# Grouping two high and two low matrix products at a few fixed places of every GEMM

## The chip, the cores and the metric

The kernel runs on one core of a Trainium2 chip. The metric is the device time of one execution in microseconds. Of the core's engines four matter here: TensorE, whose products are called PE and whose weight loads are called PEld in the profile; VectorE (DVE); ScalarE (ACT); and SyncE (SP), which issues the transfers of the weights.

## The reference

The reference computes one transformer-like block on 256 tokens of width 2048, in float32. Cut to its matrix products it is this:

```python
h = h + 0.5 * swiglu(rmsnorm(h, ffn1_norm), ffn1_w_in, ffn1_w_out)     # 2048 -> 2*5632 -> 2048
h = h + hybrid_mixer(rmsnorm(h, mix_norm), mix_w_in, ..., mix_w_out)   # 2048 -> 11296, 4096 -> 2048
h = h + 0.5 * swiglu(rmsnorm(h, ffn2_norm), ffn2_w_in, ffn2_w_out)
gate = sigmoid(rmsnorm(h, ple_norm) @ ple_w_gate)                      # 2048 -> 2048
h = h + gate * (p @ ple_w_proj)                                        # 256 -> 2048
return rmsnorm(h, final_norm)
```

Inside the mixer there are short convolutions, a gate and a state-space scan in two chunks of 128 tokens; their products are few beside those of the large weights.

## The kernel before, in words

Activations lie with the features on the 128 partitions and the 256 tokens along the row. Every float32 operand of a large product is split in two numbers of the type fp32r: a high part, which is the operand rounded, and a low part, which is what the rounding left over. An activation tile has the high part in columns 0 to 255 and the low part in columns 256 to 511 (the tiles `xa`, `xb`, `ga`, `gb`, `ya`, `yb`). A weight tile is split by the function `parts` into two tiles, `hi` (ScalarE copies, line 99) and `lo` (VectorE subtracts, line 100), for KC = 4 contraction tiles of 128 rows and 256 output columns at a time; such a piece is called a chunk.

The class `Gemm` does all large products. Its accumulator `acc` has two banks, one for each half j of the 256 output columns. For one contraction tile k and one half j there are two products, and each loads its own 128 by 128 weights first:

- the high product, `hi` weights times all 512 columns of the activation tile, into the 512 columns of the bank;
- the low product, `lo` weights times the 256 high columns, into the bank's columns 256 to 511.

The helper `gather` adds the two halves of the bank afterwards. The method `chunk` walks j on the outside and the four k inside, so TensorE sees a high and a low product in strict alternation, a pair for each k. One `Gemm` over 16 contraction tiles has 32 pairs. In the whole program there are 6,384 such pairs: 88 calls over 16 tiles in the two feed-forward input products, 44 in the mixer's input product, one of half width for dt, 48 calls over 15 or 14 tiles in the feed-forward output products, 8 over 32 tiles in the mixer's output product and 7 over 16 tiles in the gate. In a last gate tile and in the small product `pr` (the argument `one`), the products are all 256 columns wide: high weights times the high columns, high weights times the low columns, low weights times the high columns.

Between calls stand a few small products in plain float32: `nps` sums a norm over the partitions (four products with one moving column, line 183), and `npb` spreads the result over the partitions (four products, line 210).

A scheduler orders the instructions of each engine by the program and by priorities; `parts` has a raised priority. TensorE takes its instructions in that order.

Of the kernel before, what the change touches and what calls it, by code (L numbers as in the profile page):

```python
# [15 lines left out]
T = 256  # L16
# [9 lines left out]
KC = 4  # L26
# [23 lines left out]
def block_kernel(ctx, tc, xT, pT, small, dtp, w1, o1, wm, wdt, om, w2, o2, wg, wp, out):  # L50
    nc = tc.nc
# [11 lines left out]
    def aux(name):  # L63
        return aux_p.tile([P, 512], F32, tag="aux", name=name)
# [28 lines left out]
    def parts(src, nk, cols):  # L93
        w = raw.tile([P, KC, 256], F32, tag="w", name="w")
        nc.sync.dma_start(out=w[:, :nk, :cols], in_=src)
        hi = wsp.tile([P, KC, 256], F32R, tag="hi", name="hi")
        lo = wsp.tile([P, KC, 256], F32R, tag="lo", name="lo")
        with tc.high_priority(44):
            A.copy(out=hi[:, :nk, :cols], in_=w[:, :nk, :cols])  # L99
            V.tensor_tensor(out=lo[:, :nk, :cols], in0=w[:, :nk, :cols],  # L100
                            in1=hi[:, :nk, :cols].bitcast(F32), op=ALU.subtract)
        return hi, lo

    class Gemm:

        def __init__(self, src, K, rhs, cols=256, one=False, acc=None):
            self.src, self.K, self.rhs, self.cols, self.one = src, K, rhs, cols, one
            self.acc = acc_p.tile([P, 2, 512], F32, tag="acc", name="acc") if acc is None else acc  # L110

        def chunk(self, k0, k1):
            hi, lo = parts(self.src[:, k0:k1, :], k1 - k0, self.cols)
            for j in range(self.cols // P):
                js = slice(j * P, (j + 1) * P)
                for k in range(k0, k1):
                    x, acc = self.rhs(k), self.acc[:, j, :]
                    wh, wl = hi[:, k - k0, js], lo[:, k - k0, js]
                    if self.one:
                        todo = [(acc[:, 0:T], wh, x[:, 0:T]), (acc[:, 0:T], wh, x[:, T:]),  # L120
                                (acc[:, 0:T], wl, x[:, 0:T])]
                    else:
                        todo = [(acc, wh, x), (acc[:, T:], wl, x[:, 0:T])]
                    for n, (o, a, b) in enumerate(todo):
                        nc.tensor.matmul(o, lhsT=a, rhs=b, start=(k == 0 and n == 0),  # L125
                                         stop=(k == self.K - 1 and n == len(todo) - 1))

        def all(self):
            for k0 in range(0, self.K, KC):
# [3 lines left out]
    def gemm(*args, **kw):  # L133
        return Gemm(*args, **kw).all()
# [167 lines left out]
    n, held = 0, []  # L302
# [179 lines left out]
    for g in range(GROUPS):  # L482
        ng = Norm(512, "rg")
        for a in range(2):
            j = 4 * g + 2 * a
# [39 lines left out]
    for m in range(0, KD, 2):  # L525
        tail = m == KD - 2
        proj = lambda: gemm(wp[m // 2], 2, lambda k: px[:, k, :], one=True,
                            acc=aux("pr").rearrange("p (j t) -> p j t", j=2))
        pr = proj() if tail else None
        for q in range(2 if tail else 1):  # L530
            n = 1 if tail else 2
            acc = gemm(wg[m // 2][:, :, q * P:(q + n) * P], KD, xp, cols=n * P, one=tail)
# [98 lines left out]
```

## Time and profile before

| what | value |
|---|---|
| time, median of 3 executions | 2347.32 us (2345.47 to 2348.5) |
| time of the profiled execution | 2349.11 us |
| its span, first to last instruction | 2347.4 us |
| mean granted TensorE clock | 0.998 |
| TensorE products (PE) busy | 2328.8 us, 99% of the span, 13,340 products |
| weight loads (PEld) busy | 2014.5 us, 86% |
| VectorE busy | 1508.3 us, 64% |
| ScalarE busy | 1133.4 us, 48% |
| transfers | 429.38 MB, mean 183 GB/s |

The profiled execution's time is 1.7 us more than its span, and 1.8 us above the median. Products are pipelined: one starts before the one ahead of it has ended, so the ends overlap in the trace and the busy share of PE says only that some product was always in flight. What a product costs is read as the distance from its start to the next one's start.

### The profile page before, as it was taken

Reading aid. Unit: us, or ns where it says so; the run is one execution under the profiler, and the core shown is the slowest. Engines: PE = TensorE matmul, PEld = TensorE weight load, DVE = VectorE, ACT = ScalarE, POOL = GpSimd, SP = SyncE. Lnnn points to the kernel's source line nnn. Section 1 sums busy time; section 2 is a strip of 40 time slices with the busy share of each in tenths; the row PEclk is TensorE's granted clock in tenths of the full one; section 3 lists DMA queues with packets and bytes.
Section 4 is the critical chain, followed back from the end, with each engine's and each line's share of the span. In section 5 each row is a group of like instructions: output and inputs, shape, how many; then the busy total and the mean of one; then the engine's idle time right before and its main releaser. Section 6 shows DMA issues by size and latency. Waiting matters only on the chain.

```text
span 2347.4 us, 33616 instructions
## 1 busy us (share of the span) xinstructions
PE 2328.8 (99%) x13340; PEld 2014.5 (86%) x13340; DVE 1508.3 (64%) x1928; ACT 1133.4 (48%) x1491; POOL 11.8 (1%) x25
## 2 busy tenths in 40 slices
PE   8999999999999999999999999999999999999998
PEld 7888888888888888888888888888888888888887
DVE  7665566556667777777777655566556655666765
ACT  6444444444455555444455444444444444444553
POOL 0000000000000000000000000000000000000000
PEclk9999999999999999999999999999999999999999
DMA  7666666666666555555555666666666666666654
GB/s 237 187 186 181 190 187 187 182 189 187 188 180 191 185 184 178 158 165 163 170 169 179 186 186 184 186 185 186 186 188 187 185 186 186 189 185 180 189 182 137
DMA packets 126862, 429.38 MB, mean 183 GB/s; under 512 B 13616, under 2 KB 20016, under 8 KB 126704
## 3 DMA queue, kind: packets, MB, share of 16 engines
q1 hardware_dynamic: 126144, 426.17, 60.4%
q8 instruction: 104, 1.70, 0.3%
q10 hardware_dynamic: 480, 0.80, 0.1%
q14 instruction: 54, 0.44, 0.1%
q0 software_dynamic: 80, 0.26, 0.0%
HBM read 425.08 MB, written 2.10 MB: 182 GB/s over the span
## 4 chain that ended last, share of the span: by engine, by line
PE 99%; DVE 0%; DMA 0%; issue 0%; POOL 0%; ACT 0%; POOLq 0%; DVEq 0%
PE acc L125 97%; PE pr L125 0%; PE yp L407 0%; PE yp L410 0%; PE ab L386 0%; DMA sm<-in_small 0%; PE npb L210 0%; PE xt L362 0%; PE st L375 0%; PE nps L183 0%; POOL hw L559 0%; DVE cv L294 0%; DVE lo L100 0%; PE cb L355 0%; DVE xa L152 0%
## 5 line engine op out<-in xcount | busy, mean ns | idle before, releaser
L100 DVE TENSOR_TENSOR lo<-w,hi 128x1024 fp32r<-128x1024 f32 (+1 forms) x834 | 991.1, 1189 | 735.2 <-ACT hi L99 728.5
L99 ACT CAST hi<-w 128x1024 fp32r<-128x1024 f32 (+1 forms) x834 | 851.2, 1021 | 1054.2 <-PE acc L125 851.9
L125 PE MATMUL acc<-xa,hi 128*128 128x512 f32 (+1 forms) x2264 | 804.9, 399 | 6.3 <-DVE xa L152 6.3
L125 PE MATMUL acc<-xb,hi 128*128 128x512 f32 (+1 forms) x2264 | 800.8, 397 | 0.0
L125 PE MATMUL acc<-xb,lo 128*128 128x256 f32 x2248 | 633.3, 282 | 0.0
L125 PE MATMUL acc<-xa,lo 128*128 128x256 f32 x2248 | 632.3, 281 | 0.8 <-DVE lo L100 0.8
L125 PEld LDWEIGHTS acc<-xa,hi 128*128 128x128 f32 x2264 | 425.4, 188 | 110.8 <-ACT hi L99 6.3
L125 PEld LDWEIGHTS acc<-xb,hi 128*128 128x128 f32 x2264 | 424.3, 188 | 102.8
L125 PEld LDWEIGHTS acc<-xb,lo 128*128 128x128 f32 x2248 | 424.6, 189 | 3.1 <-issue 2.9
L125 PEld LDWEIGHTS acc<-xa,lo 128*128 128x128 f32 x2248 | 425.8, 189 | 1.7 <-DVE lo L100 1.5
L125 PE MATMUL acc<-ga,hi 128*128 128x512 f32 x768 | 273.7, 399 | 0.0
L125 PE MATMUL acc<-gb,hi 128*128 128x512 f32 x640 | 228.1, 398 | 0.0
L125 PE MATMUL acc<-ga,lo 128*128 128x256 f32 x768 | 215.8, 281 | 0.0
L125 PE MATMUL acc<-gb,lo 128*128 128x256 f32 x640 | 179.6, 281 | 0.0
L125 PEld LDWEIGHTS acc<-ga,hi 128*128 128x128 f32 x768 | 144.3, 188 | 35.9
L125 PEld LDWEIGHTS acc<-gb,hi 128*128 128x128 f32 x640 | 120.3, 188 | 30.2
L125 PEld LDWEIGHTS acc<-ga,lo 128*128 128x128 f32 x768 | 145.1, 189 | 0.0
L141 DVE SCALAR_TENSOR_TENSOR esum<-acc,elo 128x512 f32<-128x512 f32 (+1 forms) x196 | 133.7, 682 | 0.0
L125 PEld LDWEIGHTS acc<-gb,lo 128*128 128x128 f32 x640 | 120.9, 189 | 0.0
L139 ACT ACTIVATE elo<-acc 128x512 f32<-128x512 f32 (+1 forms) x196 | 115.5, 590 | 0.0
L125 PE MATMUL acc<-ya,hi 128*128 128x512 f32 x256 | 90.9, 399 | 0.0
L125 PE MATMUL acc<-yb,hi 128*128 128x512 f32 x256 | 90.9, 399 | 0.0
(142 smaller groups left out, 1133.5 us busy)
## 6 DMA issues: line engine op xcount, KB each, us to landing
w<-in_w SPq DMA_DIRECT2D x350, 512.0 KB, 4.4
w<-in_wm SPq DMA_DIRECT2D x176, 512.0 KB, 4.3
w<-in_o SPq DMA_DIRECT2D x144, 512.0 KB, 3.6
w<-in_om SPq DMA_DIRECT2D x64, 512.0 KB, 3.6
w<-in_wg SPq DMA_DIRECT2D x28, 512.0 KB, 4.6
w<-in_o SPq DMA_DIRECT2D x32, 384.0 KB, 3.6
w<-in_o SPq DMA_DIRECT2D x16, 256.0 KB, 3.5
w<-in_wp SPq DMA_DIRECT2D x8, 256.0 KB, 2.6
```

The source lines that it names most:

```text
L99: A.copy(out=hi[:, :nk, :cols], in_=w[:, :nk, :cols])
L100: V.tensor_tensor(out=lo[:, :nk, :cols], in0=w[:, :nk, :cols], in1=hi[:, :nk, :cols].bitcast(F32), op=ALU.subtract)
L125: nc.tensor.matmul(o, lhsT=a, rhs=b, start=(k == 0 and n == 0), stop=(k == self.K - 1 and n == len(todo) - 1))
L139: A.mul(out=lo[:, :n, :], in_=acc[:, :n, T:], mul=scale)
L141: V.scalar_tensor_tensor(out=s[:, :n, :], in0=acc[:, :n, 0:T], scalar=scale, in1=lo[:, :n, :], op0=ALU.mult, op1=ALU.add)
```

## The change

The order of the products inside a chunk is given by a string, H for the next high product and L for the next low one. As a rule it is HLHL..., as before. For the first half of the output columns (j = 0) in full chunks of four contraction tiles, it is HHLLHHLL where the chunk begins at a contraction tile divisible by 16, and HHLLHLHL where it begins 8 tiles later. The k of each product is counted separately for H and L, so the same products are summed into the same accumulator, in another order. The marks of the first and the last product of an accumulation go to the first and the last of the list.

```diff
-                for k in range(k0, k1):
-                    x, acc = self.rhs(k), self.acc[:, j, :]
-                    wh, wl = hi[:, k - k0, js], lo[:, k - k0, js]
+                order = "HL" * (k1 - k0)
+                if j == 0 and k1 - k0 == KC:
+                    order = {0: "HHLLHHLL", 8: "HHLLHLHL"}.get(k0 % 16, order)
+                todo, acc, nh, nl = [], self.acc[:, j, :], k0, k0
+                for part in order:
+                    if part == "H":
+                        k, w, nh = nh, hi, nh + 1
+                    else:
+                        k, w, nl = nl, lo, nl + 1
+                    x, a = self.rhs(k), w[:, k - k0, js]
...
-                        todo = [(acc, wh, x), (acc[:, T:], wl, x[:, 0:T])]
-                    for n, (o, a, b) in enumerate(todo):
-                        nc.tensor.matmul(o, lhsT=a, rhs=b, start=(k == 0 and n == 0),
-                                         stop=(k == self.K - 1 and n == len(todo) - 1))
+                        todo.append((acc[:, T:], a, x[:, 0:T]))
+                for n, (o, a, b) in enumerate(todo):
+                    nc.tensor.matmul(o, lhsT=a, rhs=b, start=(k0 == 0 and n == 0),
+                                     stop=(k1 == self.K and n == len(todo) - 1))
```

On TensorE, this is the start of the second `Gemm` of the program's main part (the first feed-forward tile after the norm's spread `npb`), as it stood before; xa is the activation tile of contraction tiles 0 to 7, hi_402 and lo_403 are the weights of the first chunk.

```order
L210 MATMUL npb_382<-ident_87,nrt_348 128x128 x2
L125 MATMUL acc_399<-xa_104,hi_402 128x512
L125 MATMUL acc_399<-xa_104,lo_403 128x256
L125 MATMUL acc_399<-xa_104,hi_402 128x512
L125 MATMUL acc_399<-xa_104,lo_403 128x256
L125 MATMUL acc_399<-xa_104,hi_402 128x512
```

The same place in the changed kernel, where x2 means two such products one behind the other:

```order
L220 MATMUL npb_382<-ident_87,nrt_348 128x128 x2
L135 MATMUL acc_399<-xa_104,hi_402 128x512 x2
L135 MATMUL acc_399<-xa_104,lo_403 128x256 x2
L135 MATMUL acc_399<-xa_104,hi_402 128x512 x2
L135 MATMUL acc_399<-xa_104,lo_403 128x256 x2
L135 MATMUL acc_399<-xa_104,hi_402 128x512
L135 MATMUL acc_399<-xa_104,lo_403 128x256
```

Two groups of two high and two low products now stand at the head of the call; the alternation goes on behind them with the second half of the columns. There are 608 such groups in the program.

On VectorE a few rows near the start of the dt product (the stretch about 897 us into the span) stand in another order. Before, with cv the convolution's tile and lo the low weights:

```order
L294 SCALAR_TENSOR_TENSOR cv<-esum,sm,cv 128x255
L294 SCALAR_TENSOR_TENSOR cv<-esum,sm,cv 128x253
L294 SCALAR_TENSOR_TENSOR cv<-esum,sm,cv 128x254
L100 TENSOR_TENSOR lo<-w,hi 128x1024
L294 SCALAR_TENSOR_TENSOR cv<-esum,sm,cv 128x253
```

In the changed kernel at that place:

```order
L324 TENSOR_TENSOR esum<-esum,r 128x512
L100 TENSOR_TENSOR lo<-w,hi 128x1024
L304 SCALAR_TENSOR_TENSOR cv<-esum,sm,cv 128x255 x2
L304 SCALAR_TENSOR_TENSOR cv<-esum,sm,cv 128x254 x2
```

The low weights are now made ahead of the convolution's multiplications and no longer between them. SyncE's and GpSimd's instructions stand in the same order in both kernels.

## Rows read from the trace of the kernel before

**Rows 1.** Page: span; busy time of TensorE; its granted clock in 40 slices.

```profile
span 2347.4 us, 33616 instructions
PE 2328.8 (99%) x13340; PEld 2014.5 (86%) x13340; DVE 1508.3 (64%) x1928; ACT 1133.4 (48%) x1491; POOL 11.8 (1%) x25
PEclk9999999999999999999999999999999999999999
```

**Rows 2.** Page: the chain that ended last, by engine.

```profile
PE 99%; DVE 0%; DMA 0%; issue 0%; POOL 0%; ACT 0%; POOLq 0%; DVEq 0%
```

**Rows 3.** Waits of TensorE: who waited for whom, us in total, times, longest.

```profile
PE acc L125 <- DVE xa L152: 6.3, 1, 6.3
...
PE acc L125 <- DVE lo L100: 0.8, 1, 0.8
```

**Rows 4.** Timeline of TensorE from 778.8 us: start, duration, instruction.

```profile
778.82 0.60 PE L210 MATMUL npb<-ident,nrt 128*128 128x128 f32 x4
...
779.97 0.40 PE L125 MATMUL acc<-xa,hi 128*128 128x512 f32 x1
780.21 0.28 PE L125 MATMUL acc<-xa,lo 128*128 128x256 f32 x1
780.33 0.40 PE L125 MATMUL acc<-xa,hi 128*128 128x512 f32 x1
780.56 0.28 PE L125 MATMUL acc<-xa,lo 128*128 128x256 f32 x1
780.68 0.40 PE L125 MATMUL acc<-xa,hi 128*128 128x512 f32 x1
780.91 0.28 PE L125 MATMUL acc<-xa,lo 128*128 128x256 f32 x1
781.03 0.40 PE L125 MATMUL acc<-xa,hi 128*128 128x512 f32 x1
```

**Rows 5.** Timeline of TensorE from 767.2 to 778.5 us.

```profile
767.27 0.50 PE L183 MATMUL nps<-ones,nacc 128*128 128x1 f32 x4
767.63 0.48 PE L125 MATMUL acc<-xa,hi 128*128 128x512 f32 x1
767.95 0.28 PE L125 MATMUL acc<-xa,lo 128*128 128x256 f32 x1
768.07 0.40 PE L125 MATMUL acc<-xa,hi 128*128 128x512 f32 x1
768.30 0.28 PE L125 MATMUL acc<-xa,lo 128*128 128x256 f32 x1
768.42 0.39 PE L125 MATMUL acc<-xa,hi 128*128 128x512 f32 x1
768.65 0.27 PE L125 MATMUL acc<-xa,lo 128*128 128x256 f32 x1
768.76 0.40 PE L125 MATMUL acc<-xa,hi 128*128 128x512 f32 x1
...
778.47 0.40 PE L125 MATMUL acc<-xb,hi 128*128 128x512 f32 x1
```

**Rows 6.** Line 125 by stretches: us, busy and count of products, of loads, PEclk, transfers.

```profile
32.90:767.16 734.26, 734.26 (x4158) 636.74 (x4156) 1.00 0.62 186
...
1242.84:1253.59 10.75, 10.75 (x63) 9.47 (x62) 1.00 0.62 192
1254.39:1265.33 10.94, 10.94 (x63) 9.49 (x62) 1.00 0.49 147
...
1506.30:2240.80 734.50, 734.50 (x4159) 636.88 (x4158) 1.00 0.63 186
```

**Rows 7.** Timeline of TensorE from 2320 us, in the small product `pr`.

```profile
2320.07 0.40 PE L125 MATMUL pr<-px,hi 128*128 128x256 f32 x2
2320.31 0.28 PE L125 MATMUL pr<-px,lo 128*128 128x256 f32 x1
2320.43 0.40 PE L125 MATMUL pr<-px,hi 128*128 128x256 f32 x2
```

More of the change, by code (lines that the diff above doesn't have):

```diff
@@ L115, in chunk @@
                 js = slice(j * P, (j + 1) * P)
-                for k in range(k0, k1):
-                    x, acc = self.rhs(k), self.acc[:, j, :]
-                    wh, wl = hi[:, k - k0, js], lo[:, k - k0, js]
+                order = "HL" * (k1 - k0)
[8 more added lines that the diff above has]
+                    x, a = self.rhs(k), w[:, k - k0, js]
                     if self.one:
-                        todo = [(acc[:, 0:T], wh, x[:, 0:T]), (acc[:, 0:T], wh, x[:, T:]),
-                                (acc[:, 0:T], wl, x[:, 0:T])]
-                    else:
-                        todo = [(acc, wh, x), (acc[:, T:], wl, x[:, 0:T])]
-                    for n, (o, a, b) in enumerate(todo):
-                        nc.tensor.matmul(o, lhsT=a, rhs=b, start=(k == 0 and n == 0),
-                                         stop=(k == self.K - 1 and n == len(todo) - 1))
+                        todo += [(acc[:, 0:T], a, x[:, i:i + T]) for i in ((0, T) if part == "H" else (0,))]
+                    elif part == "H":
+                        todo.append((acc, a, x))
+                    else:
+                        todo.append((acc[:, T:], a, x[:, 0:T]))
+                for n, (o, a, b) in enumerate(todo):
+                    nc.tensor.matmul(o, lhsT=a, rhs=b, start=(k0 == 0 and n == 0),
+                                     stop=(k1 == self.K and n == len(todo) - 1))
         def all(self):
```

## The prediction

> **What bounds the kernel now.** I read the page first. A product is in flight for 99% of the span, and the granted clock is full in every slice [rows 1]. The chain of waits lies to 99% on TensorE [rows 2]. The table of waits then says whether TensorE starves: its longest wait for tiles of the large products is 6.3 us, once, at the start, and it waited for low weights 0.8 us, once [rows 3]. So neither transfers nor ScalarE nor VectorE sets the time; only the distance from one product's start to the next does. A product more or less in another engine is worth nothing, and a nanosecond per pair is worth 6.4 us over the 6,384 pairs.
>
> That distance is read from the timeline, and the reader should see that it has two patterns. From 779.97 us three pairs take 781.03 - 779.97 = 1.06 us: the highs start 0.36, 0.35 and 0.35 us apart, and this goes on with period three [rows 4]. The mean is 353.3 ns; I call it the long beat. From 768.07 to 778.47 us thirty pairs take 10.40 us, 346.7 ns each; the highs start 0.35 and 0.34 us apart in turn, period two [rows 5]. This is the short beat. The same instructions, tiles and clock stand in both. Lined up by stretches: 734.26 us with 4,158 products, two of which began before the stretch, are 2,078 pairs of 353.3 ns; the stretch from 1506 us gives the same; a mixer tile of 31 pairs takes 10.75 us at 1242 us (346.8 ns) and the next one 10.94 us (353 ns, the first pairs still settling) [rows 6].
>
> A beat, once begun, lasts until something else than the alternation goes through TensorE: 2,078 pairs without a change [rows 6]. What changes it is a short interruption. Behind the four `nps` products the short beat follows [rows 5], eight times of eight in the timeline; behind the four `npb` products the long one [rows 4], nine times of nine. Transfers differ between neighbouring stretches without order (192 and 147 GB/s, [rows 6]), and the pattern does not react to what VectorE or ScalarE begin beside it. So the beat looks like a state of TensorE's own pipeline, entered by the phase in which a run of alternating products begins. What the mechanism is, no row says.
>
> **The change, part by part.** It adds and removes no instruction; 608 groups HHLL replace two pairs each. Three prices follow.
>
> (a) The group itself. Inside it two neighbours are new: high after high, low after low. The trace of before has neither for these widths. A high product is followed after 0.23 us at least [768.42 to 768.65, rows 5] and 0.24 us at most [779.97 to 780.21, rows 4]; a low one after 0.11 us [768.65 to 768.76, rows 5] to 0.12 us. For low after low the nearest row is the small product: products of 256 columns into the same columns, three in 0.36 us, 0.12 us each whichever weights they have [rows 7]. So a group takes between 2 x 0.23 + 2 x 0.11 = 0.68 us and 2 x 0.24 + 2 x 0.12 = 0.72 us, against 0.7067 us for two pairs at the long beat: -0.027 to +0.013 us each, -16 to +8 us over 608. I take two pairs at the short beat, 0.693 us, because 0.12 us per 256 columns and the rest of 346.7 ns for the high one fit both [rows 5] and [rows 7]: -8 us. Weight loads don't decide here: HLHL and HHLL both have two loads behind a high and two behind a low product. If a load were not hidden, the price is that of [rows 5]: the first high product behind `nps` holds the next for 767.95 - 767.63 = 0.32 us, 0.09 us more than usual.
>
> [...]
>
> (b) The beat behind the group. This is the larger term: pairs now on the long beat that go over to the short one save 353.3 - 346.7 = 6.67 ns. The four uninterrupted long stretches and the pieces between 898 and 1313 us hold about 5,850 of the 6,384 pairs on the long beat (about 390 are on the short one, the rest stand at seams). All of them at the short beat, groups included: 5,850 x 6.67 ns = 39 us. How many go over? A group is an interruption that comes twice in every 32 pairs, at fixed places, with 12 and 14 pairs between. The short beat has period two, and 32 pairs are 16 periods: it meets a group at the same point each time, so if it outlives one call it outlives all. The long beat has period three, and 32 is 10 periods and two pairs: it meets the groups at another point in each of three calls, so it has three tries to be knocked out. If one of them leads to the short beat, and the short beat survives, nearly the whole program ends there. I take four fifths of 39 us, 31 us, for settling pairs behind each group (two pairs settle behind `nps`, [rows 5]) and for the calls behind each `npb`.
>
> (c) The seams. In the dt stretch low weights are now made ahead of the convolution's multiplications, and a call's first low product comes one high product later. Both ease the single wait of 0.8 us [rows 3]: -0.2 to -0.8 us; I take -0.5. In the first two calls, paced by the arriving input, a group stands only at tile 8, so its two high products need two activation tiles at once; bounded by one product, under 0.3 us. The chunk's tiles are released by the second half of the columns, whose order is unchanged, so the casts and the transfers come no later.
>
> Sum: the profiled execution has 2349.1 us, of which 1.7 lie outside the span, and is 1.8 us above the median; I carry the difference over to the median. 2347.3 - 31 - 0.5 = 2316 us.
>
> **Rivals.**
>
> *The beat changes at one group and changes back at the next.* For it: 16 or so of some 50 interruptions in the whole trace are followed by the short beat, the rest by the long one, so a group need not be kind. With one third to two thirds of the pairs on the short beat the gain is 13 to 26 us: 2321 to 2334 us.
>
> *Same order, same time.* The groups pass through as two pairs, and the beat falls back to the long one behind each. For it: the only interruptions made of fp32r products alone, twelve products of `pr` ahead of a gate tile, are followed by the long beat all six times. The time is 2347 us, give or take the 3 us that the seams and the lost short stretches (390 x 6.67 ns = 2.6 us) make.
>
> *Slower: low after low costs.* The second low product adds to columns that the first has just written, and its weights have only a low product's time to load. In [rows 7] the same holds and nothing is lost, but those products are all of one width. If each group loses the upper bound of (a), 8 us, with the short stretches lost as well, it is 2347 + 8 + 3 = 2358 us; if a load stands bare in each group (0.09 us as in [rows 5]), 608 x 0.09 = 55 us: 2402 us. It decides from 8 ns a group on (4.7 us over 608), as long as the beat is not changed.
>
> **How the numbers follow.** Chances: short beat for most of the program 0.42 (own range 2305 to 2324 us), changing back and forth 0.24, same 0.17, slower 0.17. About 0.2%, 4.7 us, is what a measurement of this kernel can tell from no change. Faster by more than that: 0.42 + 0.24 = 0.66. Same: 0.17. Slower: 0.17. The range goes from 2305 us (all pairs on the short beat, 2308, and a third of what the lower bound in (a) leaves below it) to 2352 us (the groups' own cost up to 8 ns), which leaves out the dearer part of the slower case, about 0.12, and gains beyond the short beat, about 0.06.
>
> **What would show it.** In the changed kernel's timeline the highs behind a group should start 0.35 and 0.34 us apart in turn, and the windows of the feed-forward stages should hold about 346.7 ns a pair. In the group, high to high should be 0.23 to 0.24 us and low to low 0.12 us, and the four together about 0.69 us. The dt stretch should show no wait of 0.8 us. The prediction is wrong if 0.36 still comes every third pair behind the groups, if low to low is well over 0.12 us, or if the clock row shows anything but full speed.

## The result and the profile after

The changed kernel takes 2328.57 us (median of 4, 2327.06 to 2329.21) where the kernel before takes 2347.47 us: a ratio of 0.992, 95% interval 0.9902 to 0.9937. It is faster by 18.9 us. (The two profiled executions, 2349.11 and 2327.06 us, lie above and below these medians, so their spans differ by 22.1 us.) The time lies in the stated range, but at the place of the first rival, "the beat changes at one group and changes back at the next" (2321 to 2334 us), and not at the 2316 us of the case called likeliest.

The page of the changed kernel, with the three lines that answer to [rows 1]: the span is 22.1 us shorter, and neither the busy shares nor the clock tell why.

```profile
span 2325.3 us, 33620 instructions
PE 2307.8 (99%) x13340; PEld 2003.8 (86%) x13340; DVE 1507.0 (65%) x1928; ACT 1133.6 (49%) x1491; POOL 11.8 (1%) x25
PEclk9999999999999999999999999999999999999999
```

The table of TensorE's waits, which answers to [rows 3] (who waited for whom, us in total, times, longest). The wait of 0.8 us for low weights is gone, as term (c) said; the first wait is 5.7 us instead of 6.3, the next one is the same as before.

```profile
PE acc L135 <- DVE xa L162: 5.7, 1, 5.7
PE nps L193 <- ACT sq L181: 2.0, 1, 2.0
...
```

The timeline of TensorE in the changed kernel, first around the two groups at the head of a call, then around the single group at tile 8 of the same call. A row with x2 is two such products, its duration that of both together.

```profile
109.42 0.40 PE L135 MATMUL acc<-xb,hi 128*128 128x512 f32 x1
...
109.78 0.62 PE L135 MATMUL acc<-xa,hi 128*128 128x512 f32 x2
110.25 0.40 PE L135 MATMUL acc<-xa,lo 128*128 128x256 f32 x2
110.48 0.63 PE L135 MATMUL acc<-xa,hi 128*128 128x512 f32 x2
110.95 0.39 PE L135 MATMUL acc<-xa,lo 128*128 128x256 f32 x2
111.18 0.40 PE L135 MATMUL acc<-xa,hi 128*128 128x512 f32 x1
...
111.53 0.39 PE L135 MATMUL acc<-xa,hi 128*128 128x512 f32 x1
...
111.87 0.40 PE L135 MATMUL acc<-xa,hi 128*128 128x512 f32 x1
...
115.34 0.62 PE L135 MATMUL acc<-xb,hi 128*128 128x512 f32 x2
115.80 0.40 PE L135 MATMUL acc<-xb,lo 128*128 128x256 f32 x2
116.03 0.40 PE L135 MATMUL acc<-xb,hi 128*128 128x512 f32 x1
...
116.39 0.40 PE L135 MATMUL acc<-xb,hi 128*128 128x512 f32 x1
...
116.75 0.40 PE L135 MATMUL acc<-xb,hi 128*128 128x512 f32 x1
...
117.09 0.40 PE L135 MATMUL acc<-xb,hi 128*128 128x512 f32 x1
```

Read the starts of the highs. Behind the two groups they go 111.18, 111.53, 111.87: 0.35 and 0.34 us apart, the short beat. Behind the single group they go 116.03, 116.39, 116.75, 117.09: 0.36 us stands there, the long beat (the starts are rounded to 0.01 us; the means below are firmer). The groups themselves: 110.48 - 109.78 = 0.70 us and 116.03 - 115.34 = 0.69 us.

The view by stretches, for line 135 in the changed kernel (columns as in [rows 6]): the 12 pairs behind the two groups and the 14 behind the single one, in two calls one after the other, then two stretches of 600 us inside the feed-forward parts.

```profile
111.18:115.34 4.16, 4.16 (x26) 3.64 (x25) 1.00 0.64 212
116.03:120.98 4.95, 4.95 (x30) 4.29 (x29) 1.00 0.65 201
122.38:126.54 4.16, 4.16 (x26) 3.63 (x25) 1.00 0.59 206
127.23:132.19 4.95, 4.95 (x30) 4.29 (x29) 1.00 0.66 201
...
100.00:700.00 600.00, 600.00 (x3432) 522.69 (x3431) 1.00 0.62 188
...
1600.00:2200.00 600.00, 600.00 (x3431) 522.70 (x3431) 1.00 0.63 187
```

12 pairs in 4.16 us are 346.7 ns each; 14 in 4.95 us are 353.6 ns. So each of these two calls is short in one part and long in the other. Over 600 us, 3,432 products were counted, two of which had begun before: 1,715 pairs of 349.9 ns, against 353.3 ns in [rows 6]. The difference of 3.4 ns times 6,384 pairs is 22 us, about the whole change of the span.

### The profile page after: what moved, and what is told of

Read it like the earlier page. It is cut to its first block, busy times and chain, and to the rows that moved or that the text cites. A ratio compares the mean times of both kernels' runs of the same rounds, so it can differ in the third digit from the quotient of the medians.

```text
span 2325.3 us, 33620 instructions
## 1 busy us (share of the span) xinstructions
PE 2307.8 (99%) x13340; PEld 2003.8 (86%) x13340; DVE 1507.0 (65%) x1928; ACT 1133.6 (49%) x1491; POOL 11.8 (1%) x25
## 4 chain that ended last, share of the span: by engine, by line
PE 99%; DVE 0%; DMA 0%; ACT 0%; POOL 0%; issue 0%; DVEq 0%; POOLq 0%
PE acc L135 97%; PE pr L135 0%; PE yp L417 0%; PE yp L420 0%; PE ab L396 0%; PE npb L220 0%; DVE h L574 0%; PE xt L372 0%; PE st L385 0%; PE nps L193 0%; DMA sm<-in_small 0%; PE cb L365 0%; DVE xa L162 0%; POOL nrt L212 0%; PE dtT L432 0%; PE cs L441 0%
## 5 line engine op out<-in xcount | busy, mean ns | idle before, releaser
L135 PE MATMUL acc<-xb,hi 128*128 128x512 f32 (+1 forms) x2264 | 788.5, 396 | 0.0
L135 PE MATMUL acc<-xa,hi 128*128 128x512 f32 (+1 forms) x2264 | 774.0, 395 | 5.7 <-DVE xa L162 5.7
L135 PE MATMUL acc<-xb,lo 128*128 128x256 f32 x2248 | 609.7, 282 | 0.0
L135 PE MATMUL acc<-xa,lo 128*128 128x256 f32 x2248 | 580.2, 278 | 0.0
L135 PEld LDWEIGHTS acc<-xb,hi 128*128 128x128 f32 x2264 | 413.6, 188 | 88.4
L135 PEld LDWEIGHTS acc<-xa,hi 128*128 128x128 f32 x2264 | 405.5, 188 | 80.8 <-ACT hi L99 5.7
L135 PE MATMUL acc<-ga,hi 128*128 128x512 f32 x768 | 264.3, 396 | 0.0
L135 PE MATMUL acc<-ga,lo 128*128 128x256 f32 x768 | 198.4, 279 | 0.0
L135 PE MATMUL acc<-gb,lo 128*128 128x256 f32 x640 | 170.6, 279 | 0.0
L135 PEld LDWEIGHTS acc<-ga,hi 128*128 128x128 f32 x768 | 137.3, 188 | 26.1
```

Of the source, the lines that this page charges most:

```text
L135: nc.tensor.matmul(o, lhsT=a, rhs=b, start=(k0 == 0 and n == 0), stop=(k1 == self.K and n == len(todo) - 1))
```

## The experiments

Theory A: TensorE's alternating stream has two lasting beats, and a group is one of the things that turn it from one to the other. Theory B, the rival: a group is cheaper by itself and for a few pairs behind it, so the gain goes by the number of groups. All edits are to the changed kernel's line that picks the order.

**Two groups only.**

```diff
-                    order = {0: "HHLLHHLL", 8: "HHLLHLHL"}.get(k0 % 16, order)
+                    order = {0: "HHLLHHLL"}.get(k0 % 16, order)
```

> Only the two groups at contraction tile 0 of every 16 are kept (HHLLHHLL); the single group at tile 8 is alternating again. Theory A (a group turns the beat over, long to short or short to long, and the beat then stays): two groups in a row leave a short beat short, so nearly all pairs end on the short beat: about 2309 us, 2306 to 2316. Theory B (a group is cheaper by itself and for a few pairs behind it, with nothing lasting, so the gain goes by the number of groups: 19 us over 608 groups, 31 ns each): 404 groups give 12.6 us, 2335 us.

Measured: 2314.47 us (2313.81 to 2317.72), ratio 0.9868 (0.9833 to 0.9903). A third of the groups left out makes the kernel 14 us faster than the changed one. By stretches:

```profile
100.00:700.00 600.00, 600.00 (x3461) 524.52 (x3460) 1.00 0.63 189
1600.00:2200.00 600.00, 600.00 (x3462) 524.48 (x3461) 1.00 0.64 189
```

3,459 products in 600 us are 346.9 ns a pair: in these stretches the feed-forward parts are wholly on the short beat. B is out. The time is at the upper end of what A gave, because some 640 pairs, mostly in the scan and the gate, stayed long.

**The single group only.**

```diff
+                    order = {8: "HHLLHLHL"}.get(k0 % 16, order)
```

> Only the single group at contraction tile 8 of every 16 is kept (HHLLHLHL); tile 0 alternates. Theory A: one group in every call turns the beat over once, so calls end short and long in turn and about half the pairs are on the short beat: about 2327 us, 2322 to 2332. Theory B: 203 groups of 31 ns give 6 us, 2341 us.

Measured: 2331.88 us (2331.49 to 2332.15), ratio 0.9936 (0.9917 to 0.9954). As A said, about half: in its timeline the calls mostly end short and long in turn, and in 600 us there are 3,428 products, 350.1 ns a pair. But of 112 groups that met the long beat, 22 left it long (14 of them in the calls over 14 tiles), and the time is at the upper end of what A gave.

```profile
100.00:700.00 600.00, 600.00 (x3430) 522.45 (x3429) 1.00 0.63 187
```

**One group behind each spread of a norm.** `kick` is a list that `spread` appends to and the next group clears.

```diff
-                if j == 0 and k1 - k0 == KC:
-                    order = {0: "HHLLHHLL", 8: "HHLLHLHL"}.get(k0 % 16, order)
+                if j == 0 and k1 - k0 == KC and k0 % 16 == 8 and kick:
+                    order = "HHLLHLHL"
+                    kick.clear()
```

> One single group (HHLLHLHL) only, in the first chunk at contraction tile 8 that follows each spread of a norm (npb): some eight groups in the whole program, everything else alternates as before. Theory A: each of the long undisturbed stretches (2,078 pairs in either feed-forward part, 512 in the mixer's output) goes over to the short beat with its one group and stays there: about 4,660 pairs by 6.67 ns, 31 us, so 2316 us, 2312 to 2326 if one of the stretches is missed. Theory B: eight groups of 31 ns are nothing, 2347 us.

Measured: 2318.95 us (2315.80 to 2332.64), ratio 0.9894 (0.9854 to 0.9935). By the median, and in three of its four executions, eight groups give more than the change's 608. The timeline shows the first of them, and the view by stretches what stands before and behind it in both feed-forward parts:

```profile
38.04 0.63 PE L138 MATMUL acc<-xb,hi 128*128 128x512 f32 x2
38.51 0.39 PE L138 MATMUL acc<-xb,lo 128*128 128x256 f32 x2
38.73 0.40 PE L138 MATMUL acc<-xb,hi 128*128 128x512 f32 x1
...
32.62:38.04 5.42, 5.42 (x33) 4.72 (x31) 1.00 0.48 170
38.62:753.45 714.83, 714.83 (x4127) 625.15 (x4125) 1.00 0.63 190
1486.42:1491.84 5.42, 5.42 (x32) 4.71 (x31) 1.00 0.64 190
1492.43:2207.25 714.82, 714.82 (x4126) 624.89 (x4125) 1.00 0.64 190
```

Four products at 38 us, and the 2,062 pairs behind them run at 346.7 ns for 715 us, where [rows 6] has 353.3 ns. One of the four executions took 2332.64 us, 14 us above the rest; that is what one feed-forward part on the long beat costs (2,062 x 6.67 ns), but that execution has no trace, so this is argued and not shown.

**One group in the whole program.** As the last one, but only the first spread appends to `kick`.

> One single group HHLLHLHL in the whole program, in the first feed-forward part, at tile 8 of the call behind the first spread of the norm. Theory A (the beat is a lasting state that a group turns over): the 2,060 or so pairs from there to the end of the part go from 353.3 to 346.7 ns, 14 us: 2334 us, 2331 to 2337. Theory B (gain by the number of groups): nothing, 2347 to 2349 us.

Measured: 2334.21 us (2331.52 to 2334.77), ratio 0.9946 (0.9932 to 0.9961). The rows show the first feed-forward part with its group, and the second one without:

```profile
32.80:38.22 5.42, 5.42 (x33) 4.71 (x31) 1.00 0.53 172
38.80:753.63 714.83, 714.83 (x4127) 624.78 (x4125) 1.00 0.63 190
...
1488.67:2223.25 734.58, 734.58 (x4159) 637.12 (x4158) 1.00 0.63 186
```

The kernel before took 2345.56 us (2344.24 to 2349.68) beside it, so the gain is 11 us where A gave 14. A stretch without a group can change its beat from one execution to the next: in the profiled execution, of 2331.52 us, nearly all of the 512 pairs of the mixer's output product ran at 346.7 ns each, where the trace of the kernel before has 353.3 ns. That is worth about 3 us, and it may be why the kernel before is spread over 5 us; this last is not shown.

**Two groups at both places.**

```diff
+                    order = {0: "HHLLHHLL", 8: "HHLLHHLL"}.get(k0 % 16, order)
```

> HHLLHHLL at contraction tile 8 too, so two groups stand at both places. Theory A with turning over at each group: an even number at each place leaves a short beat short, about 2309 us, 2306 to 2316. If not the number of groups but the place at tile 8 is what sends the beat back to long, it stays near 2328 us. Theory B: 811 groups of 31 ns, 25 us, 2322 us.

Measured: 2322.01 us (2315.41 to 2327.28), ratio 0.9895 (0.9859 to 0.9931): between the theories by its median, and wide. Its trace, of an execution of 2318.17 us, tells them apart. The feed-forward parts are short, so the place at tile 8 is not what sends the beat back:

```profile
100.00:700.00 600.00, 600.00 (x3460) 524.33 (x3459) 1.00 0.63 189
...
1313.00:1460.00 147.00, 147.00 (x837) 127.67 (x836) 1.00 0.65 187
...
1334.97 0.40 PE L135 MATMUL acc<-ya,hi 128*128 128x512 f32 x1
...
1335.32 0.63 PE L135 MATMUL acc<-ya,hi 128*128 128x512 f32 x2
...
1336.71 0.40 PE L135 MATMUL acc<-ya,hi 128*128 128x512 f32 x1
...
1337.06 0.40 PE L135 MATMUL acc<-ya,hi 128*128 128x512 f32 x1
...
1337.42 0.40 PE L135 MATMUL acc<-ya,hi 128*128 128x512 f32 x1
```

3,458 products are 347.0 ns a pair there, but the mixer's output product at 1313 us, 835 products, stays at 352.1 ns. Counted in the timeline where at least four alternating pairs stand on either side, two groups in a row leave the short pace short 303 times of 308 and the long one long 59 times of 62. Two turns cancel in most places; what beat a stretch has is then decided where it begins, which my expectation had left out. That also fits executions 12 us apart, of which only one has a trace.

Where two turns do not cancel, the traces tell why: what a group does to the long beat depends on the point of its period of three at which it stands. Counted in the same way over the six traces with such groups (the changed kernel's and five of these), there is no exception. Where the group's first high comes 0.36 us after the last high (109.42 to 109.78 in the changed kernel), two groups led to the short beat 120 times of 120 and a single one left it long 23 times of 23. Where it comes 0.35 us after it (1334.97 to 1335.32 here), two groups left it long 89 times of 89 and a single one led to the short beat 136 times of 136. The short beat went over to the long one at a single group 235 times of 235 and stayed at two groups 495 times of 495. Highs that stand evenly, 346 to 347 ns apart, have the short beat's mean but act the other way round: two groups made them long 14 times of 14, a single one left them short 6 times of 6. These are counts; no kernel here moved a group on purpose from one point of the period to another.

**The two halves of a group apart.**

```diff
+                    order = {0: "HHLHLHLL"}.get(k0 % 16, order)
```

> At tile 0 of every 16 the chunk runs HHLHLHLL for the first half of the columns: the doubled high and the doubled low product stand two pairs apart. Theory A with the pair of neighbours as one turn: one turn for each call, as with the single group, 2332 us (2326 to 2334). If high-high and low-low each turn the beat over, the call turns twice and keeps its beat as with two groups: nearly all short, 2309 to 2318, or nearly all long, 2345 to 2349. The timeline shows at which of the two places the beat changes. Theory B: 404 odd neighbours, between 2335 and 2341 us.

Measured: 2315.17 us (2314.94 to 2315.64), ratio 0.9868 (0.9851 to 0.9884), so the call keeps its beat. The timeline shows one such place:

```profile
1813.06 0.62 PE L135 MATMUL acc<-xa,hi 128*128 128x512 f32 x2
1813.52 0.28 PE L135 MATMUL acc<-xa,lo 128*128 128x256 f32 x1
1813.63 0.40 PE L135 MATMUL acc<-xa,hi 128*128 128x512 f32 x1
1813.86 0.28 PE L135 MATMUL acc<-xa,lo 128*128 128x256 f32 x1
1813.98 0.40 PE L135 MATMUL acc<-xa,hi 128*128 128x512 f32 x1
1814.22 0.40 PE L135 MATMUL acc<-xa,lo 128*128 128x256 f32 x2
1814.46 0.40 PE L135 MATMUL acc<-xa,hi 128*128 128x512 f32 x1
...
1814.82 0.39 PE L135 MATMUL acc<-xa,hi 128*128 128x512 f32 x1
```

Behind the doubled high the last high before the doubled low, at 1813.98, holds its low for 0.24 us, a distance that only the long beat has in [rows 4] and [rows 5]; behind the doubled low the next distance is 0.36 us and the short beat follows. At all 170 such places that lie between alternating runs and were reached on the short pace, the short beat follows. That each half turns the beat, and that here they undo each other, fits this but is argued: the two pairs between the halves are too few to tell a beat.

**Groups everywhere.**

```diff
-                if j == 0 and k1 - k0 == KC:
-                    order = {0: "HHLLHHLL", 8: "HHLLHLHL"}.get(k0 % 16, order)
+                if k1 - k0 == KC:
+                    order = "HHLLHHLL"
```

> Every full chunk runs HHLLHHLL in both halves of the columns, so hardly any alternating run is left outside the tiles of 15 and 14. This prices the group without the beat. At the 0.696 us that a group took in the changed kernel's timeline (348 ns a pair against 353.3), some 6,000 pairs save 5.3 ns each, 32 us: 2316 us, 2310 to 2324. Theory B: over 2,900 groups of 31 ns, 90 us: 2257 us. If groups in a row cost more than the first (low after low building up), it is above 2330 us.

Measured: 2319.75 us (2318.27 to 2319.90), ratio 0.9886 (0.9871 to 0.9900).

```profile
100.00:700.00 600.00, 600.00 (x3449) 523.57 (x3448) 1.00 0.63 188
```

3,447 products are 348.1 ns a pair, 0.696 us a group: 1.4 ns a pair dearer than the short beat and 5.2 ns cheaper than the long one. Low after low costs nothing more when it is repeated some 3,000 times.

**Another interruption instead of a group.** At the places of the kernel with one group for each spread, the order stays HLHL and two float32 products are added, which stand as four in the trace:

```diff
+                    ps = aux("nps")
+                    for i in range(2):
+                        nc.tensor.matmul(ps[:, i:i + 1], lhsT=ident, rhs=ones[:, 0:1], start=True, stop=True)
+                    kick.clear()
```

> No group at all. At the same some eight places as in the kernel with one group for each spread, two float32 products with one moving column are put between two pairs instead (their result is not used; four products and loads in the trace, about 0.45 us each time with the first high product behind them). Theory A in its wide form (any short interruption can leave the short beat, as the norm's sums did): 2316 us and 4 us for the added products, 2318 to 2330. Theory A in its narrow form (only high-high and low-low neighbours turn the beat over): the added products alone, 2348 to 2353 us.

Measured: 2318.89 us (2318.44 to 2319.95), ratio 0.9884 (0.9869 to 0.9899). Work was added and the kernel is 27 us faster.

```profile
37.81 0.50 PE L124 MATMUL nps<-ones,ident 128*128 128x1 f32 x4
38.17 0.48 PE L140 MATMUL acc<-xb,hi 128*128 128x512 f32 x1
38.49 0.28 PE L140 MATMUL acc<-xb,lo 128*128 128x256 f32 x1
...
32.39:37.70 5.31, 5.31 (x32) 4.60 (x30) 1.00 0.52 172
38.49:753.66 715.17, 715.17 (x4127) 625.15 (x4126) 1.00 0.63 190
```

The first high product behind them is held for 0.32 us, as behind `nps` in [rows 5], and the 2,062 pairs behind it are on the short beat. The order of high and low is thus not needed for the effect.

## Why the prediction was right in part, and where it was wrong

**What bounds the kernel.** Right. Besides 1.4 us of waits only the distance of product starts changed, and 3.4 ns a pair accounts for about the 22 us of the span. The Trainium skill, "Perfetto Trace Analysis", section Identifying the Most-Contended Engine, says that the busy time of pipelined products is a poor measure of how near TensorE is to its best and names instead the arithmetic done as a share of what the engine could do, and the busy share of the weight loads. The traces agree with the first: 99% in every kernel here, from 2314 to 2347 us. The last tells no more: 86% in every one too.

**Term (a), the group's price.** Right. 0.693 us was taken; 0.70 and 0.69 us stand in the timeline above and 0.696 us in the mean of the kernel made of groups. Two lows in a row take 0.23 us (110.25 to 110.48 above), so the rival "slower" is out, and no load stood bare.

**Term (b), the beat.** The mechanism held and the size did not. That the beat is a state which outlasts its cause is shown by the kernel with a single group: one reordering of four products, 2334.21 us. What failed is the sentence "I take four fifths of 39 us", and the assumption under it, that the short beat would survive the groups that it meets. The single group at tile 8 turned it to long in all 155 cases counted in the changed kernel's timeline; two groups at the head of a call brought the long one back to short 114 times of 139. So half of the pairs were gained, 22 us of the 39 in the profiled span. What happened is the first rival, which had a chance of 0.24; the time lies in the stated range because that range held this rival and no change beside the likeliest case.

The argument from periods was right where two groups in a row meet the short beat: with two groups only it survives 161 times of 161, and that kernel's time, 2314.47 us, is near the 2316 us that I had predicted for another one, which is no merit of the sum. The argument did not foresee that a single group does the opposite of two, and it let the long beat meet the groups at another point in each of three calls. In fact the period begins anew behind each group: with the 14 pairs that stand behind the single group in the calls over 16 tiles, the long beat met the next two groups 0.36 us after the last high 111 times of 111, the point that leads to the short beat. In the calls over 15 and 14 tiles, with 12 and 10 pairs, it met them at the other points and stayed long, 24 times of 24.

Its readings of the trace of before need three corrections, which leave the sum as it is. Seven of the `nps` places and eight of the `npb` places have alternating pairs behind them, not eight and nine. Behind four of those seven, and in the mixer tile at 1242 us, the highs stand evenly 346 to 347 ns apart, with the mean of the short beat but not its period of two. And of the six places with products of `pr` ahead of a gate tile, one has the `npb` products between.

**Term (c), the seams.** Right: the wait of 0.8 us for low weights no longer stands in the table. With two groups only, 0.4 us of it is back, so which of the two reasons given for it holds is not shown.

**The rival "same order, same time".** Out: the same products at the same clock stand 346.7 or 353.3 ns a pair, by what went before. The Trainium skill ("TensorE: Matmul & The Clock Gate", section Back-to-back issue gap) gives for an isolated product at full clock a gap of about its columns over 2.4 GHz plus 2.5 ns. An estimate from that is 215.8 + 109.2 = 325 ns for the two products; in this stream, where each has its own load, the traces show neither that figure nor a single one.

That two groups turned the long beat 114 times of 139 in the changed kernel and only 3 times of 62 with two groups at both places follows from the point of the period: in the mixer's output product of the latter, 12 pairs, four whole periods, stand between the groups, so all of them meet it at a point that leaves it long. What stays open is the mechanism inside TensorE: why there are two beats, why the point of the period decides, and what a doubled high and a doubled low each do. No run here tells that.

## What to carry to other kernels

When a loop of products runs back to back, plot the distance between starts over a long stretch before touching anything else; two means for the same instructions say that there is a state to be won, and that one well-placed interruption can be worth more than an order applied everywhere. Place such a thing where the unwanted state begins, once, and look whether a repetition undoes it: here 608 groups gave 19 us, eight gave about 30 by the median, and leaving out every third group gave 34. Such a gain depends on where in the pattern the interruption falls, so it has to be measured again after each edit nearby; the version with two groups only, 2314.47 us, is the one to keep of those tried, with the one whose halves stand apart, 2315.17 us, its equal.

## What was not expected of the hardware

At a granted clock of 1.00, which is 2.4 GHz, a stream of alternating fp32r products of 512 and 256 columns has two stable paces, 346.7 and 353.3 ns a pair, and kept either for more than 2,000 pairs. Four products of one moving column, put between two pairs, moved it for 715 us from the slower to the faster one. In one execution out of nine beside the first experiments, the unchanged kernel took 2334.76 us where the others took 2347.77 to 2349.46; 14 us is again one feed-forward part on the other beat, but without a trace of that execution it is only argued.
